# Hybrid mLSTM and sparse-attention layer on one core: four copies, products and halves put at other places or on another engine

## The chip, the core and the metric

One core of a Trainium2 chip runs the whole layer. The metric is the device time of one execution in microseconds; the time before is the median of 3 runs. The engines that matter here: TensorE (PE, products and transposes), VectorE (DVE), ScalarE (ACT), GpSimd (POOL), and SyncE (SP), which issues most DMA loads. Each takes its own instructions in the order in which the program gives them, and waits on semaphores for the others.

## The reference

One decoder layer on 512 tokens of width 1024: a normalization, one wide projection, two branches (an mLSTM with 4 heads, and a sparse attention with compressed, selected and window keys), gates that merge them, an output projection, and a gated feed-forward part with a short convolution. What the change touches:

```python
h = rmsnorm(x, norm1_w)                       # tile 0 and tile 1 of 4 token tiles
proj = h @ w_in                               # first the compressed/selected keys and values
...
qn = apply_rope(rmsnorm(nq.reshape(B, S, N_HEADS, N_DH), q_norm_w), cos, sin)
...
Dw = jnp.exp(D - m_t[..., None])
s = jnp.einsum('bhctd,bhcsd->bhcts', q, k) * Dw        # the product of scores and decays
num = isc[..., None] * ... + jnp.einsum('bhcts,bhcse->bhcte', s, v)
hm = rmsnorm(hm.transpose(0, 2, 1, 3), m_out_norm_w)
hm = hm.reshape(B, S, M_V) * jax.nn.sigmoid(mo)        # head output, "output work" of a head
```

## The kernel before

Everything that enters a large product is split in two float32r parts, a high one (a rounded copy, on ScalarE) and a low one (the difference, a subtraction); each product is then three matmuls, high by high, high by low, low by high (`mm3`, L425; `ff_mm`, `feat_group` and `up_group` spell the same out). Weights come in chunks by DMA into two raw buffers; `Weights.ensure` (L71) makes the two parts of the next half chunk in one of four buffers: the high part on ScalarE (L88), the low part on VectorE or GpSimd (L94), or by a negated copy on ScalarE (L91) and an accumulating DMA that GpSimd issues (L92). Which of these is read from the table `PLAN` (L104), where `q2_pb0` to `q2_pb3` set the low parts of the four first weight halves (1 is GpSimd, 0 is VectorE) and other entries the engine of a copy (`cp`, L230: 0 is ScalarE, 1 VectorE, 2 GpSimd).

The order on every engine is written out by hand: the program issues instructions in one sequence, and each engine keeps its part of it. Between the steps of the branches a `Filler` (L136) puts projection products, in amounts from the table (`z1`, `mc2`, `mb3` and so on, in ns of products).

The start (L607 to L657): tile 0 is normalized (`norm_s` L394 takes squares on ScalarE with a running sum, `norm_b` L402 makes the factor in a short chain between VectorE and ScalarE and multiplies on VectorE at L411). `norm_t` (L414) transposes a tile on TensorE, 4 blocks at a time into one bank, copies it out on ScalarE (L422) and subtracts for the low part on VectorE (L423). The weight halves 0 and 1 are made ahead of tile 1's squares, and these ahead of tile 0's copies; tile 1's multiply follows, then halves 2 and 3. Then four token tiles by four weight halves (L640): after the second half of each tile come the transposes of the next tile and the normalization of the one after.

The query tiles (L1212 to L1227): `rope_q` rotates one tile of 128 queries on VectorE with one product on GpSimd, and copies the result beside itself (`cp` with key `p_dupq0` to `p_dupq3`, L689). `q_transposes` (L839) transposes 8 heads in two banks (L847), copies on ScalarE (L849), and subtracts on VectorE (L850). In program order: tiles 0 and 1 rotated, then for each tile t its transposes, the rotation of tile t+2, for t=1 the scores of the compressed keys (`cmp_scores` L852: products, a ScalarE copy, a VectorE addition at L864), then value-projection products as filler with their evacuation (L715) and the weight halves of the next group, the merge gates (`gm`, L488).

The mLSTM heads (L1259 to L1286): for head h `mls_b` (L1134) forms the sums (L1139), makes the scores of head h+1 (`mls_s`), their decays (`mls_e` on VectorE, `mls_x`: exponentials on ScalarE, a causal selection on GpSimd, L1126), and the head's normalization (L1160); after filler `mls_c` (L1163) transposes the head's output, multiplies by the gate (L1169), copies (L1170) and subtracts (L1171); after more filler `mls_m` (L1129) multiplies scores by decays for head h+1 (L1131, L1132). For h=2 the filler between the last two is 0. The sums of head 3 read what `mls_m` wrote.

Of the kernel before, what the change touches and what calls it, by code (L numbers as in the profile page):

```python
# [17 lines left out]
D = 1024  # L18
# [79 lines left out]
def bcast(ap, n):  # L98
# [18 lines left out]
    "p_sc21": 0, "p_sc30": 0, "p_sc31": 1, "poolA": 2, "poolC": 0, "poolGM": 2, "poolGN": 2, "poolMO": 2,  # L117
    "poolMQK": 2, "poolMV": 0, "poolUM": 0, "poolUN": 3, "poolWO": 2, "q2_eb": 1, "q2_ex0": 0, "q2_ex1": 0,
# [10 lines left out]
def FL(key, default):  # L129
    return PLAN.get(key, default)  # L130
# [30 lines left out]
def body(ctx, tc, I, out, dbg=None):  # L161
# [26 lines left out]
    def sm(shape, name, bufs=2, dt=F32):  # L188
        return small.tile(shape, dt, name=name, tag=name, bufs=bufs)
# [10 lines left out]
    def page_r(name):  # L200
        return page(name, F32R)
# [4 lines left out]
    def s4(name, dt=F32):  # L206
        return ar.tile([P, 1024], dt, name=name, tag="s4", bufs=6)
# [4 lines left out]
    def psS(name):  # L212
        return ps.tile([P, 1024], F32, name=name, tag="s", bufs=2)

    def pt(name):
        return ps.tile([P, 512], F32, name=name, tag="pt", bufs=1)
# [4 lines left out]
    def v4(tl):  # L221
        return tl[:, :2048].rearrange("p (k t) -> p k t", t=S)
# [15 lines left out]
    W = Weights(nc, wpool, 2, 4)  # L238

    def add_tok(src, c0, n, nkt, pieces=None, split=False):  # L240
        ids = []
        for k0 in range(0, nkt, 4):
            nk = min(4, nkt - k0)
            dmas = []
            for d0, s0, m in pieces or [(0, c0, n)]:
                s = src[k0 * P:(k0 + nk) * P, s0:s0 + m].rearrange("(k p) n -> p k n", p=P)
                if split:
                    for a in range(0, nk, 2):
                        dmas.append((lambda v, d0=d0, m=m, a=a: v[:, a:a + 2, d0:d0 + m], s[:, a:a + 2]))
                else:  # L250
                    dmas.append((lambda v, d0=d0, m=m: v[:, :, d0:d0 + m], s))
            views = [lambda v, a=a: v[:, a:a + 2, :] for a in range(0, nk, 2)]
            ids += W.add((nk, n), dmas, views)
        return ids
# [6 lines left out]
    T_B = add_tok(w_in, C_KC, 512, KD, split=True)  # L261
# [53 lines left out]
    xs = [s4(f"x{t}") for t in range(NT)]  # L315
# [28 lines left out]
    def keep_warm(n):  # L344
        for k in range(n):
            pe.matmul(warm[:, 0:256], identr, identr.rearrange("p (o c) -> p o c", o=1).to_broadcast([P, 2, P]),
                      start=True, stop=True)

    nw1 = psS("nw1")
# [26 lines left out]
    def col(nm, i):  # L376
        return (vcol2 if nm.startswith("ffn") else vcol)[:, where[nm] + i:where[nm] + i + 1]

    def rstd(dst, ss, n, inv):

        v, l, t = (sm([P, 32], f"rs_{z}")[:, :n] for z in "vlt")
        dve.tensor_scalar(v, ss, inv, EPS, op0=ALU.mult, op1=ALU.add)
        act.activation(l, v, AF.Ln)
        act.activation(l, l, AF.Exp, scale=-0.5)
        dve.tensor_mul(t, l, l)
        dve.tensor_mul(t, t, v)
        dve.tensor_scalar(t, t, -0.5, 1.5, op0=ALU.mult, op1=ALU.add)
        dve.tensor_mul(dst, l, t)


    def norm_a(t, src, wrow, dst, sq=None, parts=1):
        return norm_b(norm_s(t, src, wrow, dst, sq, parts))

    def norm_s(t, src, wrow, dst, sq=None, parts=1):  # L394
        ss = sm([P, 2], "ss")
        junk = dst if sq is None else sq
        for c in range(parts):
            q = slice(c * (D // parts), (c + 1) * (D // parts))
            act.activation(junk[:, q], src[:, q], AF.Square, accum_out=ss[:, c:c + 1])
        return ss, src, wrow, dst, parts  # L400

    def norm_b(args):  # L402
        ss, src, wrow, dst, parts = args
        rs = sm([P, 1], "rs")
        if parts > 1:
            dve.tensor_add(ss[:, 0:1], ss[:, 0:1], ss[:, 1:2])
        ss = ss[:, 0:1]
        rstd(rs, ss, 1, 1.0 / D)
        for c in range(0, D, D // parts):
            q = slice(c, c + D // parts)  # L410
            dve.scalar_tensor_tensor(dst[:, q], src[:, q], rs, wrow[:, q], op0=ALU.mult, op1=ALU.mult)  # L411
        return dst

    def norm_t(t, junk, H, L, psget):  # L414
        for g in range(2):
            p = psget[g](f"pn{t}_{g}")
            for k in range(4):
                c = (g * 4 + k) * P
                pe.transpose(p[:, k * P:(k + 1) * P], junk[:, c:c + P], ident)
            pv = p[:, :512].rearrange("p (k t) -> p k t", t=P)  # L420
            hd = v4(H[g])[:, :, t * P:(t + 1) * P]
            act.activation(hd, pv, AF.Copy)  # L422
            dve.tensor_sub(v4(L[g])[:, :, t * P:(t + 1) * P], pv, hd)  # L423
# [29 lines left out]
    def tok_accs(name):  # L453
        a0, a1, s = pa(name + "0"), pa(name + "1"), psS(name + "s")
        return [a0[:, :], a1[:, :], s[:, 0:512], s[:, 512:1024]]
# [151 lines left out]
    sqj = s4("sqj")  # L607
    norm_a(0, xs[0], nw1, xs[0], sqj, 2)
    keep_warm(FL("i_wb", 0))
    W.ensure(T_B[FL("q2_eb", 1)])  # L610
    nb = FL("q2_nb", 0)
    if nb:
        n1 = norm_s(1, xs[1], nw1, xs[1], s4("sqj1"))
    norm_t(0, xs[0], hTH, hTL, (po, pt))
    keep_warm(FL("i_wc", 0))
    accB = tok_accs("aB")
    if FL("q2_nc", 0):
        norm_b(n1)
    W.ensure(T_B[1])
    if FL("q2_na", 0):  # L620
        W.ensure(T_B[2])
    if nb == 0:
        n1 = norm_s(1, xs[1], nw1, xs[1], sqj)
    if FL("q2_nc", 0) == 0:
        norm_b(n1)
    W.ensure(T_B[2])
    compress_loads()
    W.ensure(T_B[3])
# [500 lines left out]
    def mls_m(sc, ee):  # L1129
        EA, EB, et = ee  # L1130
        dve.scalar_tensor_tensor(EA, sc[0], 0.125, EA, op0=ALU.mult, op1=ALU.mult)  # L1131
        dve.scalar_tensor_tensor(EB, sc[1], 0.125, EB, op0=ALU.mult, op1=ALU.mult)  # L1132
# [30 lines left out]
    def mls_c(h, hs):  # L1163
        if h == 0:
            T["hmL"] = v4(page_r("hmL"))
        p = pt(f"mhT{h}")
        for i in range(NT):
            pe.transpose(p[:, i * P:(i + 1) * P], hs[:, i * P:(i + 1) * P], ident)
        dve.scalar_tensor_tensor(hs, p, col("m_out_norm_w", h), T["mo"][:, h, :], op0=ALU.mult, op1=ALU.mult)  # L1169
        act.activation(T["hmH"][:, h, :], hs, AF.Copy)  # L1170
        dve.tensor_sub(T["hmL"][:, h, :], hs, T["hmH"][:, h, :])  # L1171
# [82 lines left out]
    sc = mls_s(0)  # L1254
    ee = mls_e(0, sc)
# [3 lines left out]
    for h in range(4):  # L1259
        if h < 3:  # L1260
            mid = (lambda: mls_s(h + 1), lambda n: mls_e(h + 1, n), mls_x)
        else:
            mid = (lambda: None, lambda n: None, lambda n: None)
        fill(FL(f"mb{h}", 1000))
        hs, sc, ee = mls_b(h, ee[2], mid)
        if h == 3:
            fill.until(done, "GN")
            fill = Filler(up_group(F_UN, T["onH"], T["onL"], evac_un, "un", "UN", (1, 3, 6, 7)), flush)
            W.ensure(F_UN[3])
            act.preload_act_table_set("sigmoid_and_others")  # L1270
            for i in range(2):
                for z in range(2):
                    g = T["gn"][i][:, 2 * z:2 * z + 2, :]
                    act.activation(g, g, AF.Sigmoid)
        fill(FL(f"mc{h}", 5000))
        mls_c(h, hs)
        if h == 3:
            for i in range(2):
                for z in range(2):
                    fill(1300)  # L1280
                    g = T["gm"][i][:, 2 * z:2 * z + 2, :]
                    act.activation(g, g, AF.Sigmoid)
            act.preload_act_table_set(LNEXP)
        if h < 3:
            fill(FL(f"md{h}", 2000))
            mls_m(sc, ee)  # L1286
    fill.until(done, "UN")
# [364 lines left out]
```

## Time and profile before

| | |
|---|---|
| median of 3 runs | 787.01 us (786.48 to 788.13) |
| profiled execution | 786.64 us, of which the span of instructions is 784.8 us |
| TensorE busy | 773.2 us, 99% of the span |
| VectorE busy | 466.5 us, 59% |
| ScalarE busy | 374.5 us, 48% |
| GpSimd busy | 211.3 us, 27% |
| granted TensorE clock | 1.0 in the whole span |

Times in the rows are microseconds from the start of the span. In a timeline a row has the start, the time to the end of the last of its instructions, the engine, the line, the operation, the tile written and the tiles read, the sizes, and the count. A bracket gives how long the engine had been idle ahead of it, and whom it had waited for. A row of a matmul is longer than the step to the next one, since they are pipelined.

### The profile page before, as it was taken

The numbers are of one execution on the slowest core, as the hardware profiler recorded it, in microseconds if no ns is written. First come the engines' busy times: TensorE is split into PE (matmuls) and PEld (weight loads), VectorE is DVE, ScalarE is ACT, GpSimd is POOL, SyncE is SP. The second block draws the span as 40 slices with busy tenths as digits, with TensorE's granted clock in tenths as the row PEclk, the third lists the DMA queues.
The fourth block names the chain that finished last, engine by engine and source line by source line (L and its number), as shares of the span: only waits on it lengthen the run. The fifth ranks groups of instructions, "written<-read, shape, count | busy, mean of one in ns | idle before, by whom it ended". The sixth has DMA issues, their size and how long they took to land.

```text
span 784.8 us, 10544 instructions
## 1 busy us (share of the span) xinstructions
PE 773.2 (99%) x4037; PEld 640.5 (82%) x4037; DVE 466.5 (59%) x823; ACT 374.5 (48%) x631; POOL 211.3 (27%) x221
## 2 busy tenths in 40 slices
PE   7999999999999999999999999999999999999998
PEld 5798778887888888888888988888888888888886
DVE  4576785677566754566627455545555454565865
ACT  6254536744665576475624253333433333455441
POOL 4420022121111113110110027755455443200700
PEclk9999999999999999999999999999999999999999
DMA  6984059756647466643588157664554534575472
GB/s 231 288 216 141 19 99 178 126 108 108 108 82 128 89 87 143 120 100 138 137 269 282 41 205 282 235 240 174 205 215 173 187 125 160 210 273 188 147 235 88
DMA packets 93892, 129.03 MB, mean 164 GB/s; under 512 B 6512, under 2 KB 72208, under 8 KB 92433
## 3 DMA queue, kind: packets, MB, share of 16 engines
q1 hardware_dynamic: 63054, 91.64, 35.0%
q0 software_dynamic: 30784, 36.70, 22.6%
q8 instruction: 32, 0.52, 0.3%
q14 instruction: 20, 0.16, 0.1%
q10 hardware_dynamic: 2, 0.00, 0.0%
HBM read 94.79 MB, written 15.73 MB: 141 GB/s over the span
## 4 chain that ended last, share of the span: by engine, by line
PE 90%; DVE 7%; ACT 2%; issue 1%; POOL 0%; DVEq 0%; POOLq 0%
PE ff L1368 10%; PE ff L1367 10%; PE ff L1369 10%; PE P L427 4%; PE P L428 4%; PE P L426 4%; PE on L947 2%; PE ptp L936 2%; PE wo L426 2%; PE wo L427 2%; PE wo L428 2%; PE gn L488 2%; PE gn L490 2%; PE gn L489 2%; PE gm L488 1%; PE gm L490 1%
## 5 line engine op out<-in xcount | busy, mean ns | idle before, releaser
L94 DVE TENSOR_TENSOR whl<-raw,whl 128x1024 fp32r<-128x1024 f32 (+1 forms) x108 | 136.5, 1276 | 148.7 <-ACT whl L88 148.7
L88 ACT ACTIVATE whl<-raw 128x1024 fp32r<-128x1024 f32 (+2 forms) x144 | 144.8, 1012 | 126.4 <-PE ff L1369 57.2
L1367 PE MATMUL ff<-h2H,whl 128*128 128x512 f32 (+1 forms) x384 | 142.8, 372 | 0.0
L1368 PE MATMUL ff<-h2L,whl 128*128 128x512 f32 (+1 forms) x384 | 142.6, 371 | 0.0
L1369 PE MATMUL ff<-h2H,whl 128*128 128x512 f32 (+1 forms) x384 | 142.6, 371 | 0.0
L92 POOL DMA_DIRECT2D whl<-raw x34 | 47.1, 1384 | 234.9 <-ACT whl L91 183.9
L1367 PEld LDWEIGHTS ff<-h2H,whl 128*128 128x128 f32 x384 | 72.3, 188 | 12.6
L1369 PEld LDWEIGHTS ff<-h2H,whl 128*128 128x128 f32 x384 | 72.3, 188 | 12.5
L1368 PEld LDWEIGHTS ff<-h2L,whl 128*128 128x128 f32 x384 | 72.4, 188 | 12.3
L921 ACT ACTIVATE P<-sp,nmx 128x128 f32<-128x128 f32 (+3 forms) x64 | 33.1, 524 | 36.9 <-DVE nmx L912 36.5
L1419 ACT ACTIVATE ct<-ct 128x512 f32<-128x512 f32 x22 | 13.9, 632 | 54.1 <-DVE ct L1417 54.1
L912 DVE TENSOR_REDUCE nmx<-sp 128x2 f32<-128x256 f32 (+3 forms) x32 | 26.2, 818 | 18.0 <-PE sp L909 17.9
L91 ACT ACTIVATE whl<-raw 128x1024 fp32r<-128x1024 f32 x34 | 35.7, 1049 | 0.0
L426 PE MATMUL P<-whl,g 128*128 128x512 f32 x88 | 34.2, 389 | 0.0
L427 PE MATMUL P<-whl,g 128*128 128x512 f32 x88 | 34.2, 389 | 0.0
L428 PE MATMUL P<-whl,g 128*128 128x512 f32 x88 | 34.2, 389 | 0.0
L1417 DVE SCALAR_TENSOR_TENSOR ct<-ff,vcol,ct 128x511 f32<-128x511 f32 (+1 forms) x44 | 32.7, 744 | 2.2 <-ACT ct L1415 1.4
L1425 ACT ACTIVATE g<-ct 128x512 fp32r<-128x512 f32 x22 | 13.9, 632 | 37.0 <-DVE ct L1429 21.9
L235 DVE COPY P<-ptp 128x256 f32<-128x256 f32 (+1 forms) x32 | 17.7, 554 | 18.6 <-PE ptp L936 18.4
L1426 DVE TENSOR_TENSOR g<-ct,g 128x512 fp32r<-128x512 f32 x22 | 15.4, 699 | 21.9 <-ACT g L1425 21.9
L488 PE MATMUL gm<-hTH,whl 128*128 128x512 f32 x64 | 26.6, 416 | 1.0 <-DVE mv L235 1.0
L427 PE MATMUL P<-whl,sb 128*128 128x512 f32 x66 | 25.9, 393 | 0.2
(400 smaller groups left out, 1783.0 us busy)
## 6 DMA issues: line engine op xcount, KB each, us to landing
raw<-in_ffn_w_up_dram SPq DMA_DIRECT2D x22, 1024.0 KB, 5.1
whl<-raw POOLq DMA_DIRECT2D x34, 512.0 KB, 5.7
raw<-in_w_in_dram SPq DMA_DIRECT2D x16, 1024.0 KB, 5.0
st<-in_ffn_w_down_dram SPq DMA_DIRECT2D x11, 1024.0 KB, 9.0
td<-st POOLq DMA_DIRECT2D x11, 1024.0 KB, 4.1
raw<-td SPq DMA_DIRECT2D x22, 512.0 KB, 5.2
raw<-in_ffn_w_down_dram SPq DMA_DIRECT2D x11, 512.0 KB, 4.8
raw<-in_w_out_dram SPq DMA_DIRECT2D x4, 1024.0 KB, 4.9
```

Source lines behind the costliest of these rows:

```text
L88: nc.scalar.activation(h, src, AF.Copy)
L91: nc.scalar.activation(l, src, AF.Copy, scale=-1.0)
L92: nc.gpsimd.dma_start(l, src, accum_op=ALU.add)
L94: (nc.gpsimd if n in self.on_pool else nc.vector).tensor_sub(l, src, h)
L426: pe.matmul(o, aH, bH, start=start, stop=False)
L427: pe.matmul(o, aH, bL, start=False, stop=False)
L428: pe.matmul(o, aL, bH, start=False, stop=stop)
L488: pe.matmul(acc, H[:, k, :], hh, start=(k == 0), stop=False)
L921: act.activation(Pv[:, y], sv[:, y], AF.Exp, bias=nmx[:, y:y + 1], accum_out=den[:, y:y + 1])
L1367: pe.matmul(acc[:, a:b], H[:, k, :], hh, start=(k == 0), stop=False)
L1368: pe.matmul(acc[:, a:b], H[:, k, :], hl, start=False, stop=False)
L1369: pe.matmul(acc[:, a:b], L[:, k, :], hh, start=False, stop=(k == KD - 1))
```

## The change

Three places.

1. At the start, tile 0's copies out of the transposes (`norm_t(0)`) stand ahead of tile 1's squares; tile 1's multiply is issued in two pieces of 512 columns; the low part of the first weight half is made by VectorE in place of GpSimd (`q2_pb0` from 1 to 0). Switches of the order that are not used any more are gone.
2. The last query tile's copy beside itself is made by VectorE in place of ScalarE (`p_dupq3` from 0 to 1).
3. After head 2's sums, the products of scores and decays for head 3 (`mls_m`) are issued ahead of the output work of head 2 (`mls_c`), not behind it.

```diff
-    "p_dupq1": 1, "p_dupq2": 1, "p_dupq3": 0, ...
+    "p_dupq1": 1, "p_dupq2": 1, "p_dupq3": 1, ...
-    ... "q2_pb0": 1, "q2_pb1": 1, "q2_pb2": 0,
+    ... "q2_pb0": 0, "q2_pb1": 1, "q2_pb2": 0,
...
-    def norm_b(args):
+    def norm_b(args, pieces=1):
         ss, src, wrow, dst, parts = args
+        pieces = max(pieces, parts)
...
-        for c in range(0, D, D // parts):
-            q = slice(c, c + D // parts)
+        for c in range(0, D, D // pieces):
+            q = slice(c, c + D // pieces)
             dve.scalar_tensor_tensor(dst[:, q], src[:, q], rs, wrow[:, q], op0=ALU.mult, op1=ALU.mult)
...
-    W.ensure(T_B[FL("q2_eb", 1)])
-    nb = FL("q2_nb", 0)
-    if nb:
-        n1 = norm_s(1, xs[1], nw1, xs[1], s4("sqj1"))
+    W.ensure(T_B[1])
     norm_t(0, xs[0], hTH, hTL, (po, pt))
     keep_warm(FL("i_wc", 0))
     accB = tok_accs("aB")
-    if FL("q2_nc", 0):
-        norm_b(n1)
-    W.ensure(T_B[1])
-    if FL("q2_na", 0):
-        W.ensure(T_B[2])
-    if nb == 0:
-        n1 = norm_s(1, xs[1], nw1, xs[1], sqj)
-    if FL("q2_nc", 0) == 0:
-        norm_b(n1)
+    norm_b(norm_s(1, xs[1], nw1, xs[1], s4("sqj1")), 2)
     W.ensure(T_B[2])
     compress_loads()
     W.ensure(T_B[3])
...
         fill(FL(f"mc{h}", 5000))
+        if h == 2:
+            mls_m(sc, ee)
         mls_c(h, hs)
...
-        if h < 3:
+        if h < 2:
             fill(FL(f"md{h}", 2000))
             mls_m(sc, ee)
```

In the table before, `q2_eb`, `q2_nb`, `q2_nc` and `q2_na` are 1, so the order before is: halves 0 and 1, tile 1's squares, tile 0's transposes and copies, tile 1's multiply, half 2, half 3.

## Rows read from the trace of the kernel before

**Rows 1.** The page, its part on the chain of work that ended last: shares of the span by engine.

```profile
PE 90%; DVE 7%; ACT 2%; issue 1%; POOL 0%; DVEq 0%; POOLq 0%
```

**Rows 2.** The waits of TensorE over the whole span, longest first: engine, tile and line, whom it waited for, microseconds in total, times, longest. The first and the last of ten.

```profile
PE warm L346 <- DVE identr L312: 1.8, 1, 1.8
...
PE vcolp L522 <- DVE hTL L423: 0.2, 1, 0.2
```

**Rows 3.** The timeline of all engines, 0 to 23 us: the start.

```profile
7.07 1.41 DVE L411 SCALAR_TENSOR_TENSOR x<-x,rs,nw 128x512 f32<-128x512 f32 x2
...
8.40 4.69 POOL L94 TENSOR_TENSOR whl<-raw,whl 128x1024 fp32r<-128x1024 f32 x2 [6.73 <-ACT whl L88]
8.69 1.06 ACT L88 ACTIVATE whl<-raw 128x1024 fp32r<-128x1024 f32 x1 [0.37 <-DMA raw<-in_w_in_dram]
...
10.03 1.06 ACT L399 ACTIVATE sqj<-x 128x1024 f32<-128x1024 f32 x1 [0.28 <-PE pn L419]
...
11.08 1.07 ACT L422 ACTIVATE hTH<-pn 128x512 fp32r<-128x512 f32 x2
11.69 1.29 DVE L423 TENSOR_TENSOR hTL<-pn,hTH 128x512 fp32r<-128x512 f32 x2 [3.22 <-ACT hTH L422]
...
11.71 0.50 PE L426 MATMUL aB<-whl,hTH 128*128 128x512 f32 x1 [1.47 <-ACT hTH L422]
...
12.90 0.14 DVE L382 TENSOR_SCALAR rs_v<-ss 128x1 f32<-128x1 f32 x1
...
14.31 1.28 DVE L411 SCALAR_TENSOR_TENSOR x<-x,rs,nw 128x1024 f32<-128x1024 f32 x1
...
15.51 2.39 DVE L94 TENSOR_TENSOR whl<-raw,whl 128x1024 fp32r<-128x1024 f32 x2
...
15.74 1.06 PE L419 MATMUL pn<-ident,x 128*128 128x128 f32 x8 [0.74 <-DVE x L411]
...
20.87 1.28 DVE L411 SCALAR_TENSOR_TENSOR x<-x,rs,nw 128x1024 f32<-128x1024 f32 x1
...
22.30 1.07 PE L419 MATMUL pn<-ident,x 128*128 128x128 f32 x8
```

**Rows 4.** The timeline of all engines, 102 to 117 us: the query tiles and the first product of the merge gates.

```profile
105.47 0.43 DVE L235 COPY qdup<-qdup 128x512 f32<-128x512 f32 x1
...
107.69 1.03 PE L847 MATMUL pq<-ident,qdup 128*128 128x128 f32 x8
...
109.66 0.69 DVE L688 TENSOR_TENSOR qdup<-rtq 128x512 f32<-128x512 f32 x1
...
110.39 0.63 ACT L233 ACTIVATE qdup<-qdup 128x512 f32<-128x512 f32 x1 [6.42 <-DVE qdup L688]
...
111.19 1.05 ACT L88 ACTIVATE whl<-raw 128x1024 fp32r<-128x1024 f32 x1
...
111.32 0.42 DVE L864 TENSOR_TENSOR vst<-sc,vst 128x256 f32<-128x256 f32 x1 [0.97 <-ACT vst L233]
...
113.08 1.07 ACT L849 ACTIVATE QS<-pq 128x512 fp32r<-128x512 f32 x2
113.11 0.39 PE L428 MATMUL aVs<-whl,hTL 128*128 128x512 f32 x1
...
113.70 1.30 DVE L850 TENSOR_TENSOR QS<-pq,QS 64x512 fp32r<-64x512 f32 x2 [1.96 <-ACT QS L849]
114.45 1.26 PE L847 MATMUL pq<-ident,qdup 128*128 128x128 f32 x8 [0.95 <-DVE QS L850]
...
116.69 0.50 PE L488 MATMUL gm<-hTH,whl 128*128 128x512 f32 x1 [0.98 <-DVE mv L235]
```

**Rows 5.** The timeline of VectorE: the same product of the rotation for the second key tile (68.31) and, beside a GpSimd product, for a query tile (93.89).

```profile
68.31 0.68 DVE L687 TENSOR_TENSOR rtk<-kraw,tab 128x512 f32<-128x512 f32 x1
...
93.89 1.23 DVE L687 TENSOR_TENSOR rtq<-qraw,tab 128x512 f32<-128x512 f32 x1
```

**Rows 6.** The timeline of all engines, 336 to 342 us: the end of head 2 and the sums of head 3.

```profile
336.16 1.13 DVE L1160 TENSOR_SCALAR hs<-mo,mrs 128x128 f32<-128x128 f32 x4
...
336.56 0.54 POOL L1126 TENSOR_SCALAR_AFFINE_SELECT EB<-EB 128x128 f32<-128x128 f32 x2
...
340.07 1.08 DVE L1131 SCALAR_TENSOR_TENSOR EA<-mA,EA 128x896 f32<-128x896 f32 x1
340.11 0.39 PE L489 MATMUL gn<-hTL,whl 128*128 128x512 f32 x1
340.34 0.39 PE L490 MATMUL gn<-hTH,whl 128*128 128x512 f32 x1
...
341.07 0.55 DVE L1132 SCALAR_TENSOR_TENSOR EB<-mB,EB 128x384 f32<-128x384 f32 x1
341.30 1.35 PE L1139 MATMUL mo<-mv,EA 128*128 128x129 f32 x10 [0.57 <-DVE EA L1131]
```

**Rows 7.** The answer on line L92, the accumulating DMAs of weight lows that GpSimd issues, 34 over the span: microseconds from issue to landing.

```profile
DMA to landing us min/median/max: 4.4/5.7/9.7
```

**Rows 8.** The timelines of ScalarE, VectorE and TensorE, 39 to 64 us: a weight copy that waited for its load, the window sums of the compressed keys (four in one row), and the first compression product.

```profile
39.59 0.68 ACT L88 ACTIVATE whl<-raw 128x576 fp32r<-128x576 f32 x1 [2.51 <-DMA raw<-in_w_in_dram]
...
60.85 2.67 DVE L779 TENSOR_TENSOR X<-pz,pet 64x496 f32<-64x496 f32 x4
...
63.77 0.40 PE L786 MATMUL ph<-cmp_k_w,X 128*64 128x256 f32 x1
```

4 rows, old and new, of the table PLAN are left out of this document.

## The prediction

> **What bounds the kernel now.** I read the views in this order. The chain that ended last is TensorE's for 90% of the span, VectorE's for 7%, ScalarE's for 2%, and holds no DMA at all [rows 1]: the end is set by the list of products, and time is won only where TensorE stands still. The list of TensorE's waits over the whole kernel has ten entries, from 1.8 us down to 0.2 us, 7.5 us in sum [rows 2]; the change can touch the five that lie in three places. The timeline of each place shows who is late there.
>
> First place, the start: the first product (11.71) waited 1.47 us for ScalarE's copy of the transposed first token tile, and that copy (11.08) stood behind the squares of the second tile (10.03), which were themselves held until the transposes had ended [rows 3]. A little later the second tile's transposes (15.74) waited 0.74 us for its normalization (14.31) [rows 3]. Second place, the query tiles: the last tile's transposes (114.45) waited 0.95 us and the first gate product (116.69) 0.98 us, both for VectorE [rows 4]. The chain runs through ScalarE there: the last query copy (110.39) had kept ScalarE idle for 6.42 us, because ScalarE takes its queue in order and the copy's source came from VectorE only at 110.35; behind it stood the score copy, a weight half's two copies (from 111.19) and the copy of query tile 2 (113.08), whose transposes had been done since about 108.7 (107.69 and 1.03) [rows 4]. Third place, the last mLSTM head: its sums (341.30) waited 0.57 us for the product at 340.07 [rows 6].
>
> **Start, step by step.** The copies of tile 0 now come straight after the copy of weight half 1, which ends at 8.69 + 1.06 = 9.75; the first can start there and the second at about 10.3, just after the transposes' end at 10.03. The first product came 0.63 us after the start of its copy (11.08 to 11.71), so it moves from 11.71 to 10.38: 1.33 us earlier [rows 3]. It needs the low of weight half 0 for the product after it. That low goes from GpSimd (half of 4.69 us, so ready at about 10.75) to VectorE, behind the first tile's multiplies that end at 7.07 + 1.41 = 8.48: at half of 2.39 us it is done at 9.7. Nothing else is in VectorE's queue then, as the first tile's lows need the copy at 9.75; so it costs nothing. GpSimd now starts half 1's low at 9.75 and ends at 12.1; the eighth product, seven steps of 0.23 us and two short waits after the first, wants it at about 12.4, a cover of 0.3 us [rows 3, 6].
>
> The squares move back to 10.8 and end with their read at 12.0 (1.06 and about 0.2). VectorE has finished the tile's two lows (1.29 us) by about 11.65, so it takes up the sum at 12.02 instead of 12.90; before, it was those lows, running until 12.98, that held the sum. From the sum to the multiply is 1.41 us (12.90 to 14.31): the multiply starts at 13.43. Two halves cost 1.41 us instead of one piece of 1.28 (the first tile's pair against the second tile's single), so they end at 14.14 and 14.84, where the one piece ended at 15.59; transposes can begin at the first [rows 3]. VectorE's next work, the lows of halves 2 and 3 (15.51), starts 0.75 us earlier. The third tile's normalization ends at 20.87 + 1.28 = 22.15 on this same VectorE queue, and its transposes (22.30) follow at once [rows 3]. So of the 1.33 us, what is late next is VectorE, and I carry 0.75 us on. Bounds: 1.33 us if VectorE doesn't hold the third tile, 0.25 us by rival A below. I take 0.75, as the third tile's transposes stand right behind VectorE.
>
> **Last query copy, step by step.** On VectorE the same copy took 0.43 us for tile 2 (105.47) [rows 4]. It runs from 110.39 to 110.82, where VectorE had 0.97 us of idle time ahead of the score addition (111.32, 0.42 us), so it delays nothing there: the addition follows, and the lows of query tile 2 start at about 111.3 instead of 113.70 [rows 4], provided ScalarE is ahead. It is: without its 6.42 us of waiting, the score copy and the weight half's two copies (1.9 us, 111.19 to 113.08) fit between 104 and 107, and the copy of tile 2 follows its transposes at about 108.5, 1.1 us long. From the lows' start to the gate product were 2.99 us (113.70 to 116.69: lows, maximum, subtraction, evacuation of the first value tile) [rows 4]; that now ends at 114.3. TensorE arrives at the transposes at 113.50 less a drain, with the tile's bank free since about 112, and at the gate product about 1.0 us after. Both gaps close: 0.95 + 0.98, and twice the drain of a product that nothing follows, 0.16 us (0.39 us long against steps of 0.23, 340.11 to 340.34 [rows 6]). That is 2.25 us. Bounds: 0 (the gaps stay) and 2.25. The weight half's accumulating DMA goes out earlier with its copies; it is queued on GpSimd behind the rope product of query tile 3 and so not before about 109.
>
> **Head 3's products, step by step.** The products' inputs are done when GpSimd's second selection ends at 336.56 + 0.54 = 337.10, and VectorE is free at 336.16 + 1.13 = 337.29. Before, head 2's output work (which waits for transposes and for ScalarE's copy) stood between, and the first product began at 340.07. Placed first, the two products (1.08 and 0.55 us) take 337.3 to 338.9. TensorE would be at the sums at 340.34 + 0.23 = 340.57 instead of 341.30: 0.73 us [rows 6]. Head 2's output is 0.8 to 0.9 us later for it, and with it ScalarE's copy of that output and the weight copy and the last gate's evacuation queued behind. Nobody wants the output before the up-projection, and its bank is read by about 339.6, ahead of the sums. Bounds: 0 and 0.73; I take 0.73.
>
> **Sum.** 0.75 + 2.25 + 0.73 = 3.73 us. The profiled execution took 786.64 us (784.8 us span and 1.84 around it), so 782.9; it lies 0.37 under the median of the runs, 787.01, so the median should come to 783.3. Nothing after the three places takes it back by the chain: no DMA ends last anywhere, and the loads are released by engines that move along.
>
> **Rivals.**
> A, the start's gain is swallowed. ScalarE's copy at 39.59 waited 2.51 us for a weight load, which does not move with TensorE, and the work on the keys is queued behind it. The compression products (63.77) start only 0.25 us after the last of the window sums that they need (60.85 + 2.67 = 63.52) [rows 8]. If that VectorE chain keeps its time, 0.25 us of the 0.75 is left: 3.23 us, 783.8. Against it: ScalarE had caught up with TensorE before the key work began.
> B, the query gaps stay, because ScalarE's copy of tile 2 is held by something that I don't see (the weight half's buffer, its load): 1.48 us are left, 785.5. Against: the idle time ahead of the query copy is put down to VectorE alone, and the half's own copies ran without a wait [rows 4].
> C, VectorE and GpSimd collide at the start. A 512-wide product of two tiles took 0.68 us alone and 1.23 us beside a GpSimd product [rows 5]. If GpSimd's low of half 1 came first, VectorE's low of half 0 would stand behind its 2.35 us, end at 13.3, and the lows of tile 0 and the second tile's sum behind it: the multiply would end near 17.4 instead of 15.59, a loss of 1.8 us where I have a gain of 0.75; in all 1.2 us won, 785.8. Against: VectorE's low ends at 9.7, GpSimd's cannot start before 9.75. The Trainium skill, SBUF — State Buffer, section "Who interferes with whom", says that the two share a port pair as an exclusive lock, held for a whole instruction by whichever started first, and that two SBUF inputs are enough; by that rule this rival decides if the order turns, and the pair of rows agrees in kind.
> D, the last head's sums gain nothing, because something else (the bank, an evacuation held by ScalarE) is just behind: 3.0 us, 784.0.
> E, slower: the low of the second gate weight half lands late. Its DMA goes out earlier, into the time in which the next weight load then also runs. It is issued at about 109 and wanted some 24 products after the first gate product, 114.4 + 5.5 = 119.9, so it has 10.9 us; the longest landing of its 34 kin is 9.7, the median 5.7 [rows 7]. From 10.9 on it costs TensorE one for one, and past 14.6 us the whole gain is gone; at 18 us the kernel would stand at 790.4. Nothing in the trace comes near.
>
> **How the numbers follow.** A measurement of this kernel can tell about 0.2%, 1.6 us, from no change. All three as worked out, 783.3: 0.60. A 0.14, B 0.10, C 0.04, D 0.08, E 0.04. Faster by over 0.2% (under 785.4): the forecast, A, D and half of B, 0.87. Within 0.2%: half of B and C, 0.09. Slower: 0.04. Range: the upper bounds give 1.33 + 2.25 + 0.73 = 4.3 us, 782.7, and the lowest run lies 0.5 under the median, so 782.2 below; above, 785.5 takes in A, D and half of B.
>
> **What would show it.** In the profile after: the first product near 10.4; no wait of the second tile's transposes beyond that for its half; the third tile's transposes near 21.5; ScalarE's copy of query tile 2 right behind its transposes; no TensorE wait for the query lows or for the value evacuation; the sums of head 3 in line behind the gate products. What would prove me wrong: a new wait of the compression products at about 63 (A), the two query waits still there (B), a VectorE low of over 2 us at 8.5 (C), a wait of gate products for a weight low (E).

## The result, and the profile after

| | before | after |
|---|---|---|
| median | 787.11 us (786.48 to 788.13, 6 runs) | 782.64 us (782.3 to 783.73, 6 runs) |
| profiled execution | 786.64 us, span 784.8 us | 782.3 us, span 780.6 us |

The ratio after to before is 0.9943, with a 95% interval of 0.9931 to 0.9956. The forecast was 783.3 us, the range 782.2 to 785.5.

Lines of the changed kernel's main part have smaller numbers than before (L837 for L847, L1121 for L1131). First the waits of TensorE over its whole span, to be laid beside [rows 2]: engine, tile and line, whom it waited for, microseconds in total, times, longest.

```profile
PE warm L346 <- DVE identr L312: 1.8, 1, 1.8
PE pn L420 <- issue: 0.4, 1, 0.4
PE on L937 <- DVE P L235: 0.3, 1, 0.3
...
PE aB L428 <- DVE whl L94: 0.2, 1, 0.2
```

Seven entries are left, 3.4 us in sum, where there were ten with 7.5. Four of the five that the prediction named are gone. The fifth, the wait of the second tile's transposes (0.74 us), is left as the entry of 0.4 us, which the profile puts to "issue": it is the wait for the first piece of the multiply (the piece starts at 13.16 below and takes half of 1.41 us, the transposes start at 14.01). The entry of 0.2 us is new, a product that waits for VectorE's low of half 2. The page's shares of the chain that ended last say the same: VectorE had 7% and ScalarE 2% in [rows 1].

```profile
PE 93%; DVE 4%; issue 1%; ACT 1%; POOL 0%; DVEq 0%; POOLq 0%
```

The timeline of the start, all engines, answers to [rows 3]: start, time to the end of the last of its instructions, engine, line, operation, tiles, sizes, count.

```profile
8.32 1.22 DVE L94 TENSOR_TENSOR whl<-raw,whl 128x1024 fp32r<-128x1024 f32 x1
8.50 1.06 ACT L88 ACTIVATE whl<-raw 128x1024 fp32r<-128x1024 f32 x1 [0.24 <-DMA raw<-in_w_in_dram]
9.46 1.20 ACT L423 ACTIVATE hTH<-pn 128x512 fp32r<-128x512 f32 x2
...
9.64 2.39 POOL L94 TENSOR_TENSOR whl<-raw,whl 128x1024 fp32r<-128x1024 f32 x1 [7.97 <-ACT whl L88]
...
10.09 0.79 PE L427 MATMUL aB<-whl,hTH 128*128 128x512 f32 x1
...
10.56 1.05 ACT L399 ACTIVATE sqj<-x 128x1024 f32<-128x1024 f32 x1
...
11.73 0.15 DVE L382 TENSOR_SCALAR rs_v<-ss 128x1 f32<-128x1 f32 x1 [0.35 <-ACT sqj L399]
...
13.16 1.41 DVE L412 SCALAR_TENSOR_TENSOR x<-x,rs,nw 128x512 f32<-128x512 f32 x2
...
14.01 1.33 PE L420 MATMUL pn<-ident,x 128*128 128x128 f32 x8 [0.38 <-issue]
14.49 2.39 DVE L94 TENSOR_TENSOR whl<-raw,whl 128x1024 fp32r<-128x1024 f32 x2
...
16.77 1.06 ACT L399 ACTIVATE sqj<-x 128x1024 f32<-128x1024 f32 x1 [0.79 <-DMA x<-in_x_dram]
...
19.85 1.28 DVE L412 SCALAR_TENSOR_TENSOR x<-x,rs,nw 128x1024 f32<-128x1024 f32 x1
...
21.27 1.07 PE L420 MATMUL pn<-ident,x 128*128 128x128 f32 x8
```

ScalarE takes the copies at 9.46, straight behind the weight copy, and the first product starts at 10.09 without a wait. VectorE's two multiplies and its lows of halves 2 and 3 (13.16, 19.85, 14.49) are 1.02 to 1.15 us earlier than in [rows 3], and so are the third tile's transposes (1.03 us). The bracket at 16.77 is new: the squares of tile 2 now wait for that tile's load.

The timeline of the query tiles, to be laid beside [rows 4]:

```profile
104.62 1.05 ACT L91 ACTIVATE whl<-raw 128x1024 fp32r<-128x1024 f32 x1
...
107.36 1.09 ACT L839 ACTIVATE QS<-pq 128x512 fp32r<-128x512 f32 x2 [1.69 <-PE pq L837]
...
109.44 0.43 DVE L235 COPY qdup<-qdup 128x512 f32<-128x512 f32 x1
109.89 0.42 DVE L854 TENSOR_TENSOR vst<-sc,vst 128x256 f32<-128x256 f32 x1
110.35 1.30 DVE L840 TENSOR_TENSOR QS<-pq,QS 64x512 fp32r<-64x512 f32 x2
...
112.40 1.03 PE L837 MATMUL pq<-ident,qdup 128*128 128x128 f32 x8
...
113.34 0.50 PE L489 MATMUL gm<-hTH,whl 128*128 128x512 f32 x1
```

The idle time of 6.42 us ahead of the copy is gone: ScalarE has done the weight half by 105.7 and waits only for the transposes (1.69 us). VectorE runs through from the copy to the lows, and neither the transposes nor the first gate product has a bracket.

The timeline of head 2's end, to be laid beside [rows 6]:

```profile
333.86 1.08 DVE L1121 SCALAR_TENSOR_TENSOR EA<-mA,EA 128x896 f32<-128x896 f32 x1
...
334.86 0.55 DVE L1122 SCALAR_TENSOR_TENSOR EB<-mB,EB 128x384 f32<-128x384 f32 x1
...
337.23 1.28 PE L1129 MATMUL mo<-mv,EA 128*128 128x129 f32 x10
```

The first product comes 6.2 us earlier and the sums, 4.07 us earlier than before, have no wait. With marks of TensorE's list from the two profiles, the gain adds up like this (us):

| mark | before | after | gained so far | in this stretch |
|---|---|---|---|---|
| third tile's transposes | 22.30 | 21.27 | 1.03 | 1.03 |
| first compression product | 63.77 | 62.80 | 0.97 | -0.06 |
| first value product | 87.29 | 86.34 | 0.95 | -0.02 |
| first gate product | 116.69 | 113.34 | 3.35 | 2.40 |
| sums of head 3 | 341.30 | 337.23 | 4.07 | 0.72 |
| first output projection product | 387.65 | 383.49 | 4.16 | 0.09 |
| span | 784.8 | 780.6 | 4.2 | 0.0 |

### The profile page after: what moved, and what is told of

Same layout as the page of the kernel before. It is cut to its first block, busy times and chain, and to the rows that moved or that the text cites. A ratio compares the mean times of both kernels' runs of the same rounds, so it can differ in the third digit from the quotient of the medians.

```text
span 780.6 us, 10546 instructions
## 1 busy us (share of the span) xinstructions
PE 773.1 (99%) x4037; PEld 641.0 (82%) x4037; DVE 468.4 (60%) x826; ACT 373.9 (48%) x630; POOL 208.1 (27%) x220
## 4 chain that ended last, share of the span: by engine, by line
PE 93%; DVE 4%; issue 1%; ACT 1%; POOL 0%; DVEq 0%; POOLq 0%
PE ff L1361 10%; PE ff L1360 10%; PE ff L1359 10%; PE P L428 4%; PE P L429 4%; PE P L427 4%; PE on L937 2%; PE ptp L926 2%; PE gn L489 2%; PE gn L491 2%; PE gn L490 2%; PE wo L429 2%; PE wo L428 2%; PE wo L427 2%; PE gm L489 1%; PE gm L491 1%
## 5 line engine op out<-in xcount | busy, mean ns | idle before, releaser
L94 DVE TENSOR_TENSOR whl<-raw,whl 128x1024 fp32r<-128x1024 f32 (+2 forms) x109 | 137.7, 1275 | 149.8 <-ACT whl L88 149.7
L92 POOL DMA_DIRECT2D whl<-raw x34 | 47.0, 1384 | 231.8 <-ACT whl L91 181.5
```

Source lines behind the costliest of these rows:

```text
L92: nc.gpsimd.dma_start(l, src, accum_op=ALU.add)
L94: (nc.gpsimd if n in self.on_pool else nc.vector).tensor_sub(l, src, h)
```

## Experiments

Twelve kernels ran, in three groups, each beside runs of the kernel before; ratios are to these, with 95% intervals. A difference of 0.001 is 0.8 us.

**The parts, one at a time.** `start_alone` is the kernel before with the first part of the change, `query_alone` with the second, `head_alone` with the third. Their edits, against the kernel before, are those hunks of the change:

```diff
# query_alone
-    "p_dupq3": 0,
+    "p_dupq3": 1,
# head_alone
+        if h == 2:
+            mls_m(sc, ee)
         mls_c(h, hs)
...
-        if h < 3:
+        if h < 2:
```

> The kernel before with the start's part of the change alone. The sum's theory: 0.75 us less, so a ratio of about 0.9990; the changed kernel's profile suggests 0.95 to 1.0 us. First product near 10.1, third tile's transposes near 21.3, the query waits (0.95 and 0.98 us) and head 3's wait (0.57) as before. Rival A (key chain anchored to a load): 0.25 us, and the compression products stay near 63.5.

> The kernel before with the last query copy on VectorE alone. The sum's theory: 2.25 us less (ratio 0.9971), both query waits gone. If the changed kernel's 2.40 us needed the earlier start as well, some 0.15 us less than that. Rival B: at least one of the two waits stays and the gain is under 1 us.

> The kernel before with head 3's products ahead of head 2's output work alone. The sum's theory: 0.73 us less (ratio 0.9991), the wait of head 3's sums gone and nothing new in its place. Rival D: no gain, with a wait for the bank or an evacuation in place of the old one.

Measured: start 0.9987 (0.9978 to 0.9996), query 0.9968 (0.9957 to 0.9979), head 0.9986 (0.9978 to 0.9995), so about 1.0, 2.5 and 1.1 us. Their product is 0.9941, the whole change's ratio 0.9943: within the intervals the parts add up, and none needs another. In `query_alone` both query waits are gone, and from the first value product to the first gate product it is 26.97 us (89.86 to 116.83) against 29.40 before and 27.00 after. In `head_alone` the sums' wait is gone and the stretch from the first gate product to the sums is 223.83 us (116.64 to 340.47) against 224.61. Rivals B and D did not happen.

`start_alone` shows something else. Its profiled execution gained nothing at the third tile (transposes at 22.35 against 22.30), because the weight halves landed late: the copies began at 8.07 and 9.40 instead of 7.26 and 8.69. And at the query waits, which it keeps, it lost more than the waits themselves. Its windows from 116 to 122 us: microseconds, busy time of each engine with its instructions, TensorE's granted clock, DMA share, GB/s.

```profile
116.00:117.00 1.00, 0.28 (x1) 0.28 (x2) 1.00 (x2) 1.00 (x2) 0.00 (x0) 0.96 1.43 179
117.00:118.00 1.00, 1.00 (x3) 0.72 (x3) 0.86 (x4) 1.00 (x2) 0.00 (x0) 0.50 1.48 196
...
120.00:121.00 1.00, 1.00 (x5) 0.77 (x5) 0.99 (x2) 0.00 (x0) 0.13 (x1) 0.83 0.24 30
121.00:122.00 1.00, 1.00 (x7) 0.78 (x6) 0.30 (x1) 0.60 (x1) 0.00 (x0) 1.00 1.45 182
```

The granted clock stood at 0.50, which is 1.2 GHz, from about 117 to just after 120 us, right behind the two waits of 0.93 and 0.97 us. TensorE's timeline there:

```profile
116.72 0.64 PE L489 MATMUL gm<-hTH,whl 128*128 128x512 f32 x1 [0.97 <-DVE mv L235]
117.16 0.63 PE L490 MATMUL gm<-hTL,whl 128*128 128x512 f32 x1
...
120.48 0.39 PE L489 MATMUL gm<-hTH,whl 128*128 128x512 f32 x1
```

The tenth gate product starts 3.76 us after the first; in the profile of before, whose clock stayed at 1.00 behind the same waits, it was 2.17 us (116.69 to 118.86). So in this execution the slow products cost 1.59 us on top of the waits. That the waits brought on the fall is not shown: the profile of `head_alone` too has both waits (0.95 and 0.98 us) and a clock of 1.00.

**What in the query part did it.** `copy_later_scalar` leaves the last query copy on ScalarE and only issues it behind the copies of query tile 2:

```diff
-        cp("p_dup" + name, 0, dst[:, :, 1, :], dst[:, :, 0, :])
+        if name != "q3":
+            cp("p_dup" + name, 0, dst[:, :, 1, :], dst[:, :, 0, :])
...
         q_transposes(t, qds[t])
+        if t == 2:
+            d3 = dup(qds[3])
+            act.activation(d3[:, :, 1, :], d3[:, :, 0, :], AF.Copy)
```

> The kernel before with the last query copy left on ScalarE, but issued behind the copies of query tile 2. Theory of the in-order queue: the cost was what stood behind the waiting copy, not the copy; most of the 2.25 us comes (1.9 to 2.4 us), and the copy, done near 111, is in time for the transposes at 113.5. Rival: the gain comes from VectorE's faster copy (0.43 against ScalarE's 0.63 us) and a shorter chain; then this kernel gains at most 0.2 us.

Measured: 0.9959 (0.9947 to 0.9971), 3.2 us and so above the expected 1.9 to 2.4, though the interval reaches down to 2.3; at least as much as `query_alone`. Its timeline:

```profile
108.72 1.09 ACT L850 ACTIVATE QS<-pq 128x512 fp32r<-128x512 f32 x2 [1.68 <-PE pq L848]
...
110.78 0.63 ACT L1219 ACTIVATE qdup<-qdup 128x512 f32<-128x512 f32 x1 [0.96 <-DVE qdup L688]
...
111.23 1.30 DVE L851 TENSOR_TENSOR QS<-pq,QS 64x512 fp32r<-64x512 f32 x2
```

The same copy, on the same engine, at the same 0.63 us, and the query lows start at 111.23 instead of 113.70; value to gate products is 26.85 us (87.69 to 114.54), 2.55 less than before. The cost was what stood behind the waiting copy in ScalarE's queue, as argued; the faster engine is not needed for the gain.

**The pieces of the start.** Four kernels are the changed kernel with one thing undone or added:

```diff
# one_piece
-    norm_b(norm_s(1, xs[1], nw1, xs[1], s4("sqj1")), 2)
+    norm_b(norm_s(1, xs[1], nw1, xs[1], s4("sqj1")))
# low0_gpsimd
-    "q2_pb0": 0,
+    "q2_pb0": 1,
# squares_first
+    n1 = norm_s(1, xs[1], nw1, xs[1], s4("sqj1"))
     norm_t(0, xs[0], hTH, hTL, (po, pt))
...
-    norm_b(norm_s(1, xs[1], nw1, xs[1], s4("sqj1")), 2)
+    norm_b(n1, 2)
# x2_early
     cs = page("cscr")
+    xload(2)
...
-    xload(2)
     xload(3)
```

> The changed kernel with tile 1's squares ahead of tile 0's copies again, all else as changed. Theory that the order carries the start's gain: the first product is 1.0 us or more later, VectorE's sum stands behind tile 0's lows, and with the same landing of the weights the third tile's transposes come 0.7 to 1.1 us later; 0.6 to 1.1 us slower than the changed kernel. Rival, that the low half on VectorE or the pieces carry it: within 0.3 us of the changed kernel.

> The changed kernel with tile 1's multiply in one piece again. Theory that VectorE is what is late next: the piece costs 1.28 instead of 1.41 us, VectorE's lows of halves 2 and 3 start 0.1 us earlier, and the third tile's transposes do not come later; within 0.15 us of the changed kernel (ratio to before near 0.994). Rival, that the first half's early transposes carry the gain: tile 1's transposes start 0.4 us later and the kernel loses 0.3 to 0.5 us.

> The changed kernel with the low of weight half 0 on GpSimd again. The two lows in series on GpSimd end near 10.7 and 13.0, so the second product waits to 10.7 and the eighth to 13.0: TensorE reaches tile 1's transposes 0.7 to 1.0 us later. If VectorE's queue sets the third tile, most of it is absorbed there: 0 to 0.4 us lost; if TensorE does, 0.7 to 1.0 us lost.

> The changed kernel with the load of token tile 2 issued ahead of the small table loads. Theory that this load is now late next at the third tile (its squares waited 0.79 us for it): the wait goes, but VectorE, free only near 18.0, takes the sum no earlier: 0 to 0.1 us gained, in a run with late weight loads up to 0.3. Rival: the load takes DMA time from the weights of halves 2 and 3, whose copies then wait: 0.3 to 0.6 us lost.

Since the weights land at other times in each execution, the marks are compared from the start of the copy of weight half 1 to the third tile's transposes. The medians come from different groups; the ratios are to the kernel before in the same group:

| kernel | half 1's copy | third tile's transposes | between | median, us | ratio to before |
|---|---|---|---|---|---|
| before | 8.69 | 22.30 | 13.61 | 787.11 | |
| after | 8.50 | 21.27 | 12.77 | 782.64 | 0.9943 |
| squares_first | 8.94 | 22.86 | 13.92 | 783.91 | 0.9950 (0.9937 to 0.9962) |
| one_piece | 8.70 | 21.93 | 13.23 | 782.76 | 0.9938 (0.9924 to 0.9951) |
| low0_gpsimd | 8.59 | 21.66 | 13.07 | 783.10 | 0.9942 (0.9930 to 0.9955) |
| x2_early | 9.50 | 22.75 | 13.25 | 782.59 | 0.9939 (0.9926 to 0.9952) |

The order carries the start's gain, by the marks: `squares_first` is 1.15 us longer in them, where 0.7 to 1.1 were expected. By the ratios it is 0.55 us longer, and the intervals overlap; but in its own group its five executions took 783.28 to 784.03 us, and those of `heads_all` below, which has the changed start, 782.43 to 783.38. In its timeline the copies come at 11.30, the first product waits 1.69 us, and VectorE's sum stands behind tile 0's lows again, as in [rows 3]:

```profile
11.91 1.29 DVE L424 TENSOR_TENSOR hTL<-pn,hTH 128x512 fp32r<-128x512 f32 x2 [2.01 <-ACT hTH L423]
13.12 0.14 DVE L382 TENSOR_SCALAR rs_v<-ss 128x1 f32<-128x1 f32 x1
```

Of the 1.15 us, 0.94 are VectorE's: tile 2's multiply starts 12.29 us after half 1's copy (21.23) instead of 11.35. The rest is TensorE's own, whose first products ran at half rate for longer (see the last section).

The low half on VectorE is worth 0.3 us by the marks of `low0_gpsimd` and nothing that timing shows. Its timeline shows where they go: with both lows on GpSimd, until 12.94, a small product in VectorE's chain for tile 1 took 0.56 us instead of 0.16 and ended together with them, and the multiply started at 13.56 instead of 13.16. It looks like the collision that `both_lows` shows below.

```profile
8.23 4.71 POOL L94 TENSOR_TENSOR whl<-raw,whl 128x1024 fp32r<-128x1024 f32 x2 [6.55 <-ACT whl L88]
12.39 0.56 DVE L385 TENSOR_TENSOR rs_t<-rs_l 128x1 f32<-128x1 f32 x1 [0.50 <-ACT rs_l L384]
```

The two pieces are worth nothing that these runs show: in `one_piece` tile 1's transposes start at 14.65 behind a wait of 0.78 us, but VectorE's lows follow 1.20 us after the multiply's start instead of 1.33, and by the clock it is the same kernel. Its longer mark (0.46 us) has another cause, in its timeline:

```profile
17.61 1.06 ACT L399 ACTIVATE sqj<-x 128x1024 f32<-128x1024 f32 x1 [1.21 <-DMA x<-in_x_dram]
```

The load of tile 2 came 0.8 us later than in the changed kernel, and TensorE then waited 0.73 us for tile 2. So that load can be on the path ahead of VectorE, and in this execution it was. `x2_early` takes the wait away (its squares start at 18.03 with no bracket), at no cost that timing shows; but its weights landed a microsecond later in the profiled execution (half 1's copy at 9.50). The earlier load alone does not bring that: in `combo` below, which has it too, the copy began at 7.98, earlier than in the changed kernel.

**Warming products.** `warm_more` puts more of them into the changed kernel, between the first tile's transposes and the first product:

```diff
-    "i_wc": 1,
+    "i_wc": 4,
```

> The changed kernel with four warming products in place of one between the first tile's transposes and the first product (some 0.9 us more of them). Theory that the half rate of the first products in several profiles (0.43 us a step instead of 0.23) follows from TensorE's idle time ahead of them: every step is 0.23 us from the start, and the time is the same to 0.5 us less, as the first product comes near 10.9. Rival, that it does not depend on that idle time: steps of 0.43 us appear again, and the time is 0 to 0.8 us more.

Measured: 783.33 us, 0.9941 (0.9929 to 0.9954). The theory fell: with no idle time ahead of the first product (10.68), the first three steps are 0.42 to 0.43 us all the same. What idle time does is below, under the hardware.

**VectorE and GpSimd at the same time.** `both_lows` adds to the changed kernel one GpSimd subtraction, of the high part of half 0 from its raw weights, that nobody reads:

```diff
-    W.ensure(T_B[1])
+    W.ensure(T_B[0])
+    pool.tensor_sub(tab[:, 0:1024].rearrange("p (a b) -> p a b", a=2),
+                    W.halves[T_B[0]][1](W.raws[W.halves[T_B[0]][0]]), W.hl[T_B[0]][0])
+    W.ensure(T_B[1])
```

> The changed kernel with an added GpSimd subtraction of the same size, on the same two inputs as VectorE's low of weight half 0, so that both run near 8.3; its output is read by nobody. Rival C's mechanism (a VectorE product of two tiles stands behind or beside a GpSimd one): VectorE's low takes 2.2 us or more instead of 1.22. If it doesn't hold, 1.22 us stay. In either case GpSimd's low of half 1 comes 1 us or so later and the eighth product waits for it: 0.3 to 1.5 us slower than the changed kernel.

Measured: 784.05 us, 0.9958 (0.9944 to 0.9972). The timelines of VectorE and GpSimd in it:

```profile
8.37 2.37 POOL L612 TENSOR_TENSOR tab<-raw,whl 128x1024 f32<-128x1024 f32 x1 [6.69 <-ACT whl L88]
8.41 3.42 DVE L94 TENSOR_TENSOR whl<-raw,whl 128x1024 fp32r<-128x1024 f32 x1
10.69 3.38 POOL L94 TENSOR_TENSOR whl<-raw,whl 128x1024 fp32r<-128x1024 f32 x1
```

VectorE's low took 3.42 us instead of 1.22 beside a GpSimd subtraction that had started 0.04 us earlier: it ended at 11.83, 1.1 us after GpSimd's end. Then it went the other way: GpSimd's next low started at 10.69 and took 3.38 us instead of 2.39. The third tile's transposes came at 22.95, 1.68 us later than in the changed kernel with the same landing of the weights (8.52 against 8.50). So rival C's mechanism exists, and in this form it costs 1.7 us by the marks (expected were up to 1.5); by the ratios the intervals overlap. The Trainium skill, SBUF — State Buffer, section "Who interferes with whom", says that the two engines share a port pair that is an exclusive lock, that a VectorE instruction with two SBUF inputs contends with a GpSimd instruction that reads SBUF, and that issue order decides who blocks; the durations here agree with that.

In the changed kernel VectorE's low ended at 9.54 and GpSimd's began at 9.64. But the distance to rival C is not that 0.1 us. `combo` (below) shows the two overlapping with VectorE first:

```profile
8.31 1.22 DVE L94 TENSOR_TENSOR whl<-raw,whl 128x1024 fp32r<-128x1024 f32 x1
9.12 2.65 POOL L94 TENSOR_TENSOR whl<-raw,whl 128x1024 fp32r<-128x1024 f32 x1 [7.45 <-ACT whl L88]
```

VectorE's low kept its 1.22 us, and only GpSimd's was longer, 2.65 instead of 2.39. For rival C GpSimd has to start first, and in the changed kernel it started 1.3 us after VectorE (9.64 against 8.32).

**Other heads, and a better version.** `heads_all` is the changed kernel with the products ahead of the output work for every head; `combo` puts the edits of `copy_later_scalar`, `one_piece` and `x2_early` into the changed kernel.

```diff
# heads_all
-        if h == 2:
+        if h < 3:
             mls_m(sc, ee)
         mls_c(h, hs)
...
         if h < 2:
             fill(FL(f"md{h}", 2000))
-            mls_m(sc, ee)
```

> The changed kernel with the products of scores and decays ahead of the output work for heads 1 and 2 as well. There filler products (3.9 and 3.6 us) stand between, and the sums of heads 1 and 2 had no wait in the profile: no difference, within 0.2 us. Rival, that these products are late there too under the output work: 0.3 us or more gained.

> The changed kernel with the last query copy on ScalarE behind the copies of query tile 2, tile 1's multiply in one piece and the load of token tile 2 early. By the marks of the single runs: 0.13 us from the query part, 0.1 us from VectorE, and no wait for token tile 2; 0.1 to 0.4 us less than the changed kernel, which timing can't tell from none.

Measured: `heads_all` 782.50 us, 0.9937 (0.9924 to 0.9949), and 223.84 us from the first gate product to head 3's sums against 223.89: no difference. `combo` 781.94 us (781.79 to 782.88), 0.9930 (0.9916 to 0.9943): the lowest median of all, 0.7 us under the changed kernel's. Its interval overlaps that of the changed kernel, so that it is better is likely and not shown. Value to gate products is 26.85 us in it (86.05 to 112.90), 0.15 us less than in the changed kernel, where 0.13 were expected.

## Why the prediction was right

The sum was 3.73 us; the two profiles differ by 4.2 us (spans) and the medians by 4.47. Each of the three mechanisms was seen at work. What the profiles gained beyond the sum is mainly 0.28 us at the start, 0.15 at the query tiles and 0.09 behind the sums of head 3. The median, 782.64, lies just under the 782.7 that the prediction's upper bounds give, and is in the range by the 0.5 us that it allows for the spread of the runs.

**Start, forecast 0.75 us: the mechanism is right, the size depends on what the profile of before did not show.** The first product came at 10.09 (forecast 10.38), the sum at 11.73 (12.02), the multiply at 13.16 (13.43), the lows of halves 2 and 3 at 14.49 (15.51 less 0.75, 14.76), the third tile 1.03 us earlier. All are 0.27 to 0.29 us ahead of the forecast, and 0.19 of that is half 1's copy, which began at 8.50 instead of 8.69 as its load landed earlier. Counted from that copy the gain is 0.84 us; in the two other profiles with exactly this start it is 0.66 (`start_alone`, 9.40 to 22.35) and 0.98 (`heads_all`, 8.80 to 21.43). VectorE is what is late next in this profile, but only just: its sum for the third tile (18.00) has no idle time ahead of it, and the tile's squares, which had waited 0.79 us for a load that the prediction did not look at, were read out at 17.92. In `one_piece` the load was the later of the two. The cover of 0.3 us for the low of half 1 held (GpSimd done at 12.03, the eighth product at 12.31).

The profile of before was a good execution of the old start. Counted in the same way, `head_alone` (7.88 to 22.29), `copy_later_scalar` (8.49 to 22.69) and `query_alone` (9.87 to 24.88), which all have the old start, took 14.4, 14.2 and 15.0 us instead of 13.61. In these three TensorE's first products ran at half rate for longer than in the profile of before (last section), and the third tile's transposes come 0.3 to 0.5 us after VectorE's multiply has ended, without a wait, behind TensorE's own products; in the profile of before they follow VectorE within 0.15 us. In `head_alone`:

```profile
20.48 1.28 DVE L411 SCALAR_TENSOR_TENSOR x<-x,rs,nw 128x1024 f32<-128x1024 f32 x1
22.29 1.03 PE L419 MATMUL pn<-ident,x 128*128 128x128 f32 x8
```

So what the new start gains also depends on that rate, which the prediction took as full (steps of 0.23 us from the first product on).

One reading in the prediction does not hold: that tile 1's squares were held until the transposes had ended (10.03 in [rows 3]). In `head_alone` and `copy_later_scalar` they began at 9.22 and 9.84, ahead of the transposes' end at 10.02 and 10.03, and as in the profile of before some 0.28 us after the end of half 1's copy. What holds them for that time is open; no term of the sum uses it.

**Query copy, forecast 2.25 us, measured 2.40.** The waiting copy, what stood behind it and both waits behaved as worked out; the copy took 0.43 us and delayed nothing. The sum left out that the second four of the transposes had waited too, for the second of VectorE's two lows: the eight took 1.26 us before and 1.03 after.

**Head 3's products, forecast 0.73 us, measured 0.72**, and 0.09 more further on, 0.07 of it in the sums themselves: from the first of them to the eleventh it was 1.19 us before, behind a wait, and is 1.12 after.

**Rivals.** A: no, of 1.03 us only 0.08 were lost on the way to the value products. B and D: no. C: no; the prediction asks that VectorE's low end ahead of GpSimd's start, and `combo` shows that it is enough to start first, which it did by 1.3 us. E: the accumulating DMA went out at 108.00 and no gate product waited; the longest landing of its kin is 9.6 us after, 9.7 in [rows 7].

**What the forecast lacked** is what can come behind TensorE's waits: the 1.59 us in `start_alone`, whose profiled execution has a mean granted clock of 0.998. Beside the first group, 16 of the 23 executions of the kernel before had a mean of 0.998 or less (median 788.1 us, the other seven 787.2). Over all groups, such a mean stands at 32 of the 65 executions of the kernels that keep the two query waits (24 of 43 of the kernel before, 6 of 11 of `start_alone`, 2 of 11 of `head_alone`), and at 2 of the 58 of those that don't (one of `query_alone`, one of `both_lows`). So the waits and the falls go together, and a part of the change's gain is likely to be falls that no longer come. How large it is these runs don't say; the 0.3 us by which the medians differ more than the two spans are within the noise.

## What to carry to other kernels

An instruction that waits in an in-order queue costs what stands ready behind it and is wanted soon, not its own duration: look for a long idle bracket on an engine that is far from busy, and ask since when the next instructions could have run. Issuing it later on the same engine can be worth as much as giving it to another. Compare the start of a kernel from the moment the first loads have landed, and over several profiles; a wait of 0.2 us resolved in one profile says little when the landing moves by 2 us.

## What the runs showed of the hardware that was not expected

The clock fell to 1.2 GHz (granted 0.50) for some 3 us behind two waits of 0.93 and 0.97 us with eight transposes between them, in one profile and not in two others with the same waits (before and `head_alone`).

At the start, products ran at the same half rate though the record gives a granted clock of 1.00. The window from 14 to 15 us (columns as above) and TensorE's timeline in `head_alone`:

```profile
14.00:15.00 1.00, 1.00 (x4) 0.75 (x3) 1.00 (x2) 0.60 (x1) 0.00 (x0) 1.00 0.94 376
```

```profile
10.90 0.80 PE L426 MATMUL aB<-whl,hTH 128*128 128x512 f32 x1 [0.67 <-ACT hTH L422]
11.50 0.63 PE L427 MATMUL aB<-whl,hTH 128*128 128x512 f32 x1
11.92 0.63 PE L428 MATMUL aB<-whl,hTL 128*128 128x512 f32 x1
12.35 0.63 PE L426 MATMUL aB<-whl,hTH 128*128 128x512 f32 x1
...
15.70 0.40 PE L428 MATMUL aB<-whl,hTL 128*128 128x512 f32 x1
```

Steps are 0.43 us until about 15.5, then 0.23. In the six profiles where TensorE had no wait ahead of its first product (`after`, `one_piece`, `low0_gpsimd`, `warm_more`, `heads_all`, `combo`) the full rate came between 11.4 and 12.9 us; in five where it had waited 0.67 to 1.69 us (`start_alone`, `head_alone`, `copy_later_scalar`, `x2_early`, `squares_first`) between 14.5 and 16.4, and in `query_alone` (2.63 us) not before 18. Two don't fit: before, with a wait of 1.47 us, was at full rate by its fourth product (12.77), and `both_lows`, which had no wait ahead of its first product but one of 0.97 us ahead of its second, by the fourth as well (12.82). So idle time ahead of the first products goes with a later full rate in most profiles, and these runs don't settle what decides it.
